# Square sums behind the chain at a phase boundary, and gated tiles in parts of 4, 6, 6, 6

## The chip, the cores and the metric

The kernel runs on one core of one Trainium2 chip. The metric is the device time of one execution in microseconds (us). The engines are PE (TensorE, the matmuls), DVE (VectorE), ACT (ScalarE), POOL (GpSimd) and SP (SyncE, which issues the loads of weights). Each works through its own instructions in order, and the order is fixed when the program is built.

## The reference

Two layers, each a feed-forward block, a mixing block and a second feed-forward block. 512 new prompt positions and 8 x 4 sampled positions go through the same weights; the width is 1024, all in float32.

```
def layer(x, ...):
    h = x + 0.5 * rmsnorm(swiglu(rmsnorm(x, norms[0]), w_ffn1_up, w_ffn1_down), norms[1])
    m, s_new, buf_new = mixer(rmsnorm(h, norms[2]), ...)      # retention and a short gated convolution
    h = h + rmsnorm(m, norms[3])
    h = h + 0.5 * rmsnorm(swiglu(rmsnorm(h, norms[4]), w_ffn2_up, w_ffn2_down), norms[5])

def swiglu(x, w_up, w_down):                                  # w_up: 1024 x 5632, w_down: 2816 x 1024
    gate, up = jnp.split(x @ w_up, 2, axis=-1)
    return (jax.nn.silu(gate) * up) @ w_down

def rmsnorm(x, g):
    return x * rsqrt(mean(x * x) + 1e-6) * g
```

## The kernel before

The 544 positions are the columns of every activation, in two halves of 272 (HALF); features lie on the 128 partitions, so the width of 1024 is 8 tiles (KT) and the inner width of 2816 is 22 tiles (FT). A float32 product is made of three matmuls, high part by high part, high by low and low by high. The high parts are copies made by ACT (`whi`, `xh`, `hh`, `oh`), the low parts are differences made by DVE (`wlo`, `xl`, `hl`, `ol`).

The work is a list of jobs in 6 phases: feed-forward, mixing, feed-forward, twice over. A plain `Job` is one output tile: 8 input tiles x 3 x 2 halves, 48 matmuls. A `Pair` computes two output tiles by seven block products of 4 x 3 matmuls, 84 instead of 96. It needs operands (sums and differences of quarters of the normalized input), which `build_ops` makes in four steps, two input tiles each, on DVE and ACT. Phases therefore begin with plain jobs. In a feed-forward phase the 22 gated tiles come in parts (PARTS): the gated tiles of a part, then 8 down tiles that take the part's tiles as inputs and add to the sums so far, which are copied into the PSUM bank first (`seed`, L194). Only the first part is done plainly, so its jobs are two for each gated tile (a gate, then an up) and then 8 down jobs. BUILD_AT says behind which jobs of that list the four builds are issued.

A boundary between phases is written out by hand. `boundary` fills a script with (time, function) pairs, sorts it, and that is the order on DVE, ACT and POOL (`play`); the times are only keys of the order. The order on PE and SP is that of the program too. Everything issued outside the scripts is placed on DVE, ACT and POOL by a planner, which may put such instructions among those of a script where it expects the engine to be idle.

In a boundary the last 5 jobs of a phase (TAIL) run half by half. While the second half of them runs on PE, the first half's residual `x` is finished by a chain on DVE and ACT (`chain`): scale y (L1165), add to x (L1169), high part of the next input (L1144, ACT), low part (L1150). Then PE starts the head, the first 5 jobs (HEAD) of the next phase, half by half: three jobs interleaved over the 8 input tiles, then two whole ones (`head_part`). While PE does the first half of the head, the second half's chain runs. The head runs on inputs that are not yet normalized; its results are copied from PSUM (`copy`, L1324) and are multiplied later by the reciprocal root of the mean square. For that each half needs a sum of squares over the 8 tiles of x: a square on ACT (L442) and an add on DVE (L444, the last one L448), then a matmul with ones on PE (L469) and `rstd`: a root on ACT (L481), three operations on DVE (L482 to L484). SUMS places the squares and adds in the script, RSTD_HEAD the two roots. After the second root `rest(0)` issues the evacuations of the first half (products with r, Silu, parts); `head_side` issues those of the second. `later_prep` makes the parts of the weights for the next jobs, five times in a boundary; its second step also frees the buffer of raw weights, on which SP's next load waits (three such buffers, L229).

PSUM has 8 banks, of which matmuls use 6 in a feed-forward phase and 5 in a mixing phase. A job takes one for each half, in the order in which they were given back.

The lines that count:

```
ev(SUMS[half] + 0.45 * f, lambda f=f: self.pre_sum(nxt, f, half, None, nc.vector))   # L1180
ev(RSTD_HEAD[half], lambda half=half: self.rstd([nxt["acc"][:, self.hs(half)]], half, nxt["r"], DM))   # L1344
ev(RSTD_HEAD[1] + 0.1, lambda: rest(0))   # L1345
ev((HEAD * half + max(3, n + 1)) * d + 0.1 + 0.3 * n * (n < 3), lambda n=n, half=half: copy(n, half))   # L1330, d = 2.78
jobs[at].after = lambda k=k: self.build_ops(ph, k)   # L574, for at in BUILD_AT
```

In the second half of the head the keys are 13.88 + 1.04 k for the interleaved steps on PE, 22.21 and 24.99 for the two whole jobs, and 22.31, 22.61, 22.91, 25.09 and 27.87 for the five copies.

Of the kernel before, what the change touches and what calls it, by code (L numbers as in the profile page):

```python
# [27 lines left out]
P = 128  # L28
KT = DM // P
FT = DFF // P  # L30
PARTS = [(0, 5), (5, 10), (10, 15), (15, 22)]
PLAIN_PARTS = 1
BUILD_AT = (6, 9, 11, 13)
CONV_PLAIN = 2
BUILD_MIX = (0, 2, 4, 5)
EPS = 1e-6
# [23 lines left out]
LAST_B = 1.2  # L60
ONES_B = 4.2
CHAIN_B = 5.0
SUMS = 11.0, 19.0
URGENT = 300
RSTD_HEAD = 17.5, 22.5


def log_gammas():
# [63 lines left out]
class Trunk:  # L132
# [362 lines left out]
    def ffn_jobs(self, ph):  # L495
# [4 lines left out]
        ph["y"] = {}  # L500
        for pi, (p0, p1) in enumerate(PARTS):
            hh = {}
# [51 lines left out]
            def dn(m, pi=pi, p0=p0, p1=p1, hh=hh):  # L554
                last = pi == len(PARTS) - 1

                def mv():
                    return [hh[i] for i in range(p0, p1)]

                def ev(half, ps):  # L560
                    if pi == 0 and half == 0:
                        ph["y"][m] = self.u("y")
                    if last:
                        self.y_out(ph, m, half, ps)
                    else:
                        nc.scalar.activation(out=ph["y"][m][:, self.hs(half)], in_=ps[:, :HALF], func=AF.Copy)

                return Job(down[l, n, m, :, p0 * P:p1 * P], mv, ev,
                           seed=(lambda half: ph["y"][m][:, self.hs(half)]) if pi else None)

            jobs += [dn(m) for m in range(KT)]
        self.no_ops(ph)
        for k, at in enumerate(BUILD_AT):
            jobs[at].after = lambda k=k: self.build_ops(ph, k)  # L574
# [582 lines left out]
    def chain(self, ev, at, ph, nxt, half):  # L1157

        nc, s = self.nc, self.hs(half)
        ts = {}  # L1160
        step = STEP if nxt else 0.8

        def scale(f):
            t = ts[f] = self.t("yg")
            nc.vector.tensor_tensor(out=t, in0=ph["y"][f][:, s], in1=ph["ry"][:, s], op=ALU.mult)  # L1165

        def add(f):
            x = self.x[f][:, s]
            nc.vector.tensor_tensor(out=x, in0=x, in1=ts.pop(f), op=ALU.add)  # L1169
            if nxt is None:  # L1170
                nc.sync.dma_start(out=self.a["y"][f, :, s], in_=x)

        for f in range(KT):
            t = at + step * f
            ev(t, lambda f=f: scale(f))
            ev(t + step + 0.4, lambda f=f: add(f))
            if nxt is not None:
                ev(t + step + 0.8, lambda f=f: self.pre_hi(nxt, f, half))
                ev(t + 2 * step + 0.8, lambda f=f: self.pre_lo(nxt, f, half))
                ev(SUMS[half] + 0.45 * f, lambda f=f: self.pre_sum(nxt, f, half, None, nc.vector))  # L1180

    def finish(self, ev, ph, d):

# [52 lines left out]
    def boundary(self, ph, nxt, i):  # L1236

        nc, script = self.nc, []  # L1240

        def ev(t, fn):
            script.append((t, len(script), fn))

        self.fill()
        self.x_changed = True
        mvs = [self.jobs[i + n].mv() for n in range(TAIL)]
        d = len(mvs[0]) * 3 * MM
        tb = -d * TAIL
        banks = {}  # L1250
        self.prep(i + TAIL + 1)
        self.tc.keep_in_program_order(nc.scalar.preload_act_table(AF.Abs_reciprocal_sqrt))
        ph["ry"] = self.u("ry")

        def seed(n, half):
            banks[n, half] = self.seeds(i + n, (half,))[0][1]

        def part(n, half):
            self.run_part(i + n, half, banks[n, half], 0, RSTD_AT if (n, half) == (0, 1) else KT)

        def between():
            self.rstd([ph["yacc"][:, self.hs(0)]], 0, ph["ry"], DM)
            self.run_part(i, 1, banks[0, 1], RSTD_AT)

        for half in range(2):
            at = -d * TAIL * (2 - half)
            for n in range(TAIL):
                ev(at + d * n - 0.9 * d, lambda n=n, half=half: seed(n, half))
                ev(at + d * n, lambda n=n, half=half: part(n, half))
                ev(at + d * (n + 1) + 0.1, lambda n=n, half=half: self.evac(self.jobs[i + n], half, banks[n, half]))  # L1270
        ev(tb + RSTD_AT * 3 * MM, between)
        if nxt is not None:
            self.pre_tiles(nxt)
            ev(-0.001, lambda: self.of_mix(nxt["kind"] == "mix"))
        self.chain(ev, tb + CHAIN_A, ph, nxt, 0)
        if nxt is None:
            self.finish(ev, ph, d)
        else:
            ev(LAST_B, lambda: ph["last"].pop()())
            ev(ONES_B, lambda: self.rstd([ph["yacc"][:, self.hs(1)]], 1, ph["ry"], DM))  # L1280
            self.chain(ev, CHAIN_B, ph, nxt, 1)
            V, G = nc.vector, nc.gpsimd
            self.head_script(ev, nxt, i + TAIL)
            for hi, lo in ((tb + d + 0.3, tb + d + 1.3), (tb + 2 * d + 0.3, tb + 2 * d + 1.3), (1.0, 2.0), (6.0, 7.0),
                           (14.0, 15.0)):
                self.later_prep(ev, hi, lo, V)
        self.play(script)
        if nxt is not None:
            self.head_side(nxt)
# [23 lines left out]
    def head_script(self, ev, nxt, i0):  # L1313

        nc = self.nc
        d = KT * 3 * MM
        if nxt["kind"] == "mix":
            self.mix_start(nxt)
        banks, out = [], []

        def copy(n, half):
            if half == 0:
                out.append(self.u("out"))
            nc.scalar.activation(out=out[n][:, self.hs(half)], in_=banks[half][n][:, :HALF], func=AF.Copy)  # L1324
            self.give(banks[half][n])

        for half in range(2):
            banks.append(self.head_part(ev, half * HEAD * d, nxt, i0, half))
            for n in range(HEAD):
                ev((HEAD * half + max(3, n + 1)) * d + 0.1 + 0.3 * n * (n < 3), lambda n=n, half=half: copy(n, half))  # L1330

        def rest(half):
            todo = []
            first = (3, 4) if nxt["kind"] == "mix" else ()
            for n in (*first, *(n for n in range(HEAD) if n not in first)):
                if n == 0 and first:
                    self.mix_tables(nxt, half)
                todo.append(self.jobs[i0 + n].evac(half, out[n][:, self.hs(half)]))
            for fn in todo:
                if fn:  # L1340
                    fn()

        for half in range(2):
            ev(RSTD_HEAD[half], lambda half=half: self.rstd([nxt["acc"][:, self.hs(half)]], half, nxt["r"], DM))  # L1344
        ev(RSTD_HEAD[1] + 0.1, lambda: rest(0))  # L1345
        nxt["rest"] = rest

    def head_side(self, nxt):
# [199 lines left out]
```

## Time and profile before

| | us |
|---|---|
| median of 3 runs | 2678.73 (2677.65 to 2682.8) |
| profiled execution | 2677.17 |
| its span, first to last instruction | 2675.3 |
| PE busy | 2628.3 (98%), 20718 matmuls |
| DVE busy | 1861.0 (70%) |
| ACT busy | 1354.0 (51%) |
| POOL busy | 237.3 (9%) |

The busy time of an engine is the time in which one of its instructions runs; PE's matmuls overlap, so that only its idle time is exact. A wait is the idle time of an engine before an instruction, with the instruction whose semaphore ended it behind the arrow. The granted clock is the share of its full rate that TensorE was allowed. Phases begin their heads on PE at about 6, 387, 955, 1334, 1713 and 2283 us.

### The profile page before, as it was taken

Reading aid. Unit: us, or ns where it says so; the run is one execution under the profiler, and the core shown is the slowest. Engines: PE = TensorE matmul, PEld = TensorE weight load, DVE = VectorE, ACT = ScalarE, POOL = GpSimd, SP = SyncE. Lnnn points to the kernel's source line nnn. Section 1 sums busy time; section 2 is a strip of 40 time slices with the busy share of each in tenths; the row PEclk is TensorE's granted clock in tenths of the full one; section 3 lists DMA queues with packets and bytes.
Section 4 is the critical chain, followed back from the end, with each engine's and each line's share of the span. In section 5 each row is a group of like instructions: output and inputs, shape, how many; then the busy total and the mean of one; then the engine's idle time right before and its main releaser. Section 6 shows DMA issues by size and latency. Waiting matters only on the chain. (4 is left out here: it accounts for less than half of the span.)

```text
span 2675.3 us, 50606 instructions
## 1 busy us (share of the span) xinstructions
PE 2628.3 (98%) x20718; PEld 2606.1 (97%) x20718; DVE 1861.0 (70%) x3213; ACT 1354.0 (51%) x2546; POOL 237.3 (9%) x375
## 2 busy tenths in 40 slices
PE   9999999999999999999999999999999999999998
PEld 9999998999999999999999999999999999999997
DVE  6756748677986487667488557587678764875673
ACT  6555554434553455555555555544345434655553
POOL 1000021222100100000100000211210001000002
PEclk9999999999999999999999999999999999999999
DMA  4233344333343432332432334343333433323332
GB/s 155 83 96 102 105 142 148 116 107 120 103 132 104 133 106 83 99 103 86 130 118 84 101 95 144 114 147 105 111 116 101 130 104 121 118 83 95 102 105 90
DMA packets 91977, 296.86 MB, mean 111 GB/s; under 512 B 12064, under 2 KB 16288, under 8 KB 91744
## 3 DMA queue, kind: packets, MB, share of 16 engines
q1 hardware_dynamic: 74592, 235.46, 28.9%
q0 software_dynamic: 17152, 58.16, 6.3%
q8 instruction: 162, 2.65, 0.4%
q14 instruction: 71, 0.58, 0.1%
HBM read 266.17 MB, written 27.41 MB: 110 GB/s over the span
## 5 line engine op out<-in xcount | busy, mean ns | idle before, releaser
L324 PE MATMUL banks<-oh,whi 128*128 128x272 f32 x2040 | 588.6, 289 | 3.0 <-ACT banks L194 1.6
L324 PE MATMUL banks<-oh,wlo 128*128 128x272 f32 x2040 | 587.9, 288 | 0.0
L324 PE MATMUL banks<-ol,whi 128*128 128x272 f32 x2040 | 586.6, 288 | 0.0
L324 PE MATMUL banks<-xh,whi 128*128 128x272 f32 x1600 | 455.2, 298 | 9.6 <-ACT out L1324 8.7
L324 PE MATMUL banks<-xl,whi 128*128 128x272 f32 x1600 | 442.4, 289 | 0.0
L252 ACT ACTIVATE whi<-raw 128x1024 fp32r<-128x1024 f32 (+2 forms) x273 | 253.5, 931 | 313.3 <-PE banks L324 248.4
L256 DVE TENSOR_TENSOR wlo<-raw,whi 128x1024 fp32r<-128x1024 f32 (+2 forms) x273 | 291.2, 1068 | 150.5 <-ACT whi L252 117.6
L324 PEld LDWEIGHTS banks<-oh,whi 128*128 128x128 f32 x2040 | 383.8, 188 | 6.4 <-ACT banks L194 2.8
L324 PE MATMUL banks<-hh,whi 128*128 128x272 f32 x1408 | 385.2, 289 | 0.1
L324 PE MATMUL banks<-hl,whi 128*128 128x272 f32 x1408 | 384.5, 288 | 0.2
L324 PEld LDWEIGHTS banks<-ol,whi 128*128 128x128 f32 x2040 | 384.5, 188 | 0.0
L324 PEld LDWEIGHTS banks<-oh,wlo 128*128 128x128 f32 x2040 | 383.9, 188 | 0.0
L324 PE MATMUL banks<-xh,wlo 128*128 128x272 f32 x1600 | 371.5, 289 | 0.4 <-DVE wlo L1395 0.4
L264 DVE TENSOR_TENSOR wlo<-s,whi 128x1024 fp32r<-128x1024 f32 x204 | 249.7, 1224 | 102.8 <-ACT whi L263 50.5
L324 PEld LDWEIGHTS banks<-xh,whi 128*128 128x128 f32 x1600 | 303.4, 190 | 13.2 <-ACT out L1324 10.0
L324 PE MATMUL banks<-hh,wlo 128*128 128x272 f32 x1408 | 313.3, 288 | 0.0
L324 PEld LDWEIGHTS banks<-xl,whi 128*128 128x128 f32 x1600 | 303.4, 190 | 2.1 <-DVE xl L1150 1.0
L263 ACT ACTIVATE whi<-s 128x1024 fp32r<-128x1024 f32 x204 | 214.8, 1055 | 141.3 <-PE banks L324 97.8
L324 PEld LDWEIGHTS banks<-xh,wlo 128*128 128x128 f32 x1600 | 267.9, 190 | 1.1 <-DVE wlo L1395 1.1
L324 PEld LDWEIGHTS banks<-hh,whi 128*128 128x128 f32 x1408 | 264.9, 188 | 0.9 <-ACT banks L194 0.8
L324 PEld LDWEIGHTS banks<-hl,whi 128*128 128x128 f32 x1408 | 264.8, 188 | 0.8 <-DVE hl L547 0.6
L324 PEld LDWEIGHTS banks<-hh,wlo 128*128 128x128 f32 x1408 | 229.6, 188 | 0.0
(246 smaller groups left out, 4993.3 us busy)
## 6 DMA issues: line engine op xcount, KB each, us to landing
raw<-in_w_up SPq DMA_DIRECT2D x173, 512.0 KB, 3.6
raw<-in_w_in SPq DMA_DIRECT2D x128, 512.0 KB, 3.6
raw<-in_w_down SPq DMA_DIRECT2D x96, 320.0 KB, 3.0
raw<-in_w_down SPq DMA_DIRECT2D x32, 448.0 KB, 4.0
xd<-x POOLq DMA_DIRECT2D x40, 272.0 KB, 2.7
x<-xd POOLq DMA_DIRECT2D x40, 272.0 KB, 4.9
s<-in_state_ret POOLq DMA_DIRECT2D x32, 256.0 KB, 3.5
out_ret_s<-s POOLq DMA_DIRECT2D x32, 256.0 KB, 2.9
```

The costliest lines, as they stand in the source:

```text
L252: self.nc.scalar.activation(out=hi[:, :n], in_=r[:, :n], func=AF.Copy)
L256: eng.tensor_tensor(out=lo[:, :n], in0=r[:, :n], in1=hi[:, :n].bitcast(F32), op=ALU.subtract)
L263: self.nc.scalar.activation(out=hi, in_=r, func=AF.Copy)
L264: self.nc.vector.tensor_tensor(out=lo, in0=r, in1=hi.bitcast(F32), op=ALU.subtract)
L324: self.nc.tensor.matmul(out=ps[:, :HALF], lhsT=w, rhs=x, start=start, stop=stop, skip_group_check=again)
```

## The change

The square sums of both halves, until now at 11.0 to 14.2 and 19.0 to 22.2 in the boundary's script, move to 17.6 to 18.0 and 18.2 to 18.6, that is behind the last step of the second half's chain (17.5). The fifth preparation of weights moves from 14.0 and 15.0 to 18.7 and 18.8. The first half's root moves from 17.5 to 18.3 and so behind one more step on PE; the second half's from 22.5 to 22.1 and so ahead of the two whole head jobs, and `rest(0)` from 22.6 to 22.15, ahead of the copy at 22.31. The parts of gated tiles become 4, 6, 6 and 6 instead of 5, 5, 5 and 7, the first of them plain; and the builds follow jobs 5, 6, 8 and 9 of a phase instead of 6, 9, 11 and 13.

```diff
@@ -28,9 +28,9 @@
-PARTS = [(0, 5), (5, 10), (10, 15), (15, 22)]
+PARTS = [(0, 4), (4, 10), (10, 16), (16, 22)]
 PLAIN_PARTS = 1
-BUILD_AT = (6, 9, 11, 13)
+BUILD_AT = (5, 6, 8, 9)
@@ -60,9 +60,9 @@
-SUMS = 11.0, 19.0
+SUMS = 17.6, 18.2
 URGENT = 300
-RSTD_HEAD = 17.5, 22.5
+RSTD_HEAD = 18.3, 22.1
@@ -1177,7 +1177,7 @@
-                ev(SUMS[half] + 0.45 * f, lambda f=f: self.pre_sum(nxt, f, half, None, nc.vector))
+                ev(SUMS[half] + 0.05 * f, lambda f=f: self.pre_sum(nxt, f, half, None, nc.vector))
@@ -1282,7 +1282,7 @@
             for hi, lo in ((tb + d + 0.3, tb + d + 1.3), (tb + 2 * d + 0.3, tb + 2 * d + 1.3), (1.0, 2.0), (6.0, 7.0),
-                           (14.0, 15.0)):
+                           (18.7, 18.8)):
@@ -1342,7 +1342,7 @@
-        ev(RSTD_HEAD[1] + 0.1, lambda: rest(0))
+        ev(RSTD_HEAD[1] + 0.05, lambda: rest(0))
```

## Rows read from the trace of the kernel before

**Rows 1.** The page, part 1: busy us (share of the span) and instructions of each engine.
```profile
PE 2628.3 (98%) x20718; PEld 2606.1 (97%) x20718; DVE 1861.0 (70%) x3213; ACT 1354.0 (51%) x2546; POOL 237.3 (9%) x375
```
**Rows 2.** Who waited for whom on PE: us in total, times, longest us.
```profile
PE banks L469 <- DVE acc L448: 15.4, 10, 1.6
PE banks L324 <- ACT out L1324: 8.7, 6, 2.8
...
PE banks L324 <- ACT banks L194: 1.6, 3, 0.7
```
**Rows 3.** Stretches: length, busy time (instructions) of five engines, clock, DMA share, GB/s.
```profile
1050.00:1250.00 200.00, 200.00 (x1597) 200.00 (x1597) 130.90 (x186) 105.87 (x200) 0.00 (x0) 1.00 0.33 96
...
49.50:52.90 3.40, 3.40 (x17) 3.40 (x17) 3.40 (x11) 2.71 (x7) 0.00 (x0) 0.50 0.00 0
1752.80:1756.10 3.30, 3.30 (x16) 3.30 (x16) 3.24 (x10) 0.30 (x1) 0.00 (x0) 0.50 0.00 0
425.60:429.00 3.40, 3.40 (x27) 3.40 (x28) 3.31 (x9) 0.74 (x3) 0.00 (x0) 1.00 0.02 6
```
**Rows 4.** Timeline of PE: start, length, instruction, [idle before, what ended it].
```profile
48.96 0.39 PE L324 MATMUL banks<-xh,whi 128*128 128x272 f32 x1 [2.52 <-ACT out L1324]
...
419.26 0.50 PE L469 MATMUL banks<-acc,ones 128*128 128x272 f32 x1 [1.60 <-DVE acc L448]
...
425.53 0.39 PE L324 MATMUL banks<-xh,whi 128*128 128x272 f32 x1 [2.29 <-ACT out L1324]
...
976.47 0.50 PE L469 MATMUL banks<-acc,ones 128*128 128x272 f32 x1 [1.57 <-DVE acc L448]
...
986.55 0.50 PE L469 MATMUL banks<-acc,ones 128*128 128x272 f32 x1 [1.58 <-DVE acc L448]
...
996.69 0.39 PE L324 MATMUL banks<-xh,whi 128*128 128x272 f32 x1 [0.40 <-ACT out L1324]
...
1744.41 0.50 PE L469 MATMUL banks<-acc,ones 128*128 128x272 f32 x1 [1.58 <-DVE acc L448]
...
1751.24 0.39 PE L324 MATMUL banks<-xh,whi 128*128 128x272 f32 x1 [2.83 <-ACT out L1324]
```
**Rows 5.** Timeline of DVE in the second boundary.
```profile
965.90 0.50 DVE L1150 SCALAR_TENSOR_TENSOR xl<-x,par,xh 128x272 fp32r<-128x272 f32 x1
...
967.01 0.50 DVE L1150 SCALAR_TENSOR_TENSOR xl<-x,par,xh 128x272 fp32r<-128x272 f32 x1
...
975.97 0.44 DVE L448 SCALAR_TENSOR_TENSOR acc<-sq,acc 128x272 f32<-128x272 f32 x1 [0.75 <-ACT sq L442]
...
981.85 3.17 DVE L444 TENSOR_TENSOR acc<-acc,sq 128x272 f32<-128x272 f32 x6
```
**Rows 6.** Timeline of ACT in the second boundary.
```profile
979.73 2.34 ACT L442 ACTIVATE sq<-x 128x272 f32<-128x272 f32 x7
...
991.88 1.28 ACT L513 ACT_TABLE_LOAD   x1
993.17 0.75 ACT L513 ACTIVATE sg<-sg 128x272 f32<-128x272 f32 x2
...
996.26 1.24 ACT L1324 ACTIVATE out<-banks 128x272 f32<-128x272 f32 x4
```
**Rows 7.** Timeline of DVE behind that boundary: a build, and the last plain job.
```profile
1001.24 0.78 DVE L587 SCALAR_TENSOR_TENSOR n<-x,par,r 128x544 f32<-128x544 f32 x1
...
1007.55 1.36 DVE L264 TENSOR_TENSOR ol<-t,oh 128x544 fp32r<-128x544 f32 x2
...
1020.95 0.79 DVE L520 TENSOR_TENSOR tu<-banks,r 128x272 f32<-128x272 f32 x2 [4.50 <-PE banks L324]
...
1023.10 0.79 DVE L526 TENSOR_TENSOR hl<-tu,hh 128x272 fp32r<-128x272 f32 x2
```
**Rows 8.** The stretch from that boundary's second root to the first Pair's operands.
```profile
991.10:1047.80 56.70, 56.30 (x449) 56.08 (x448) 47.56 (x97) 32.13 (x67) 0.00 (x0) 1.00 0.24 70
```
**Rows 9.** Timeline of DVE in the first boundary: the first half's last two low parts.
```profile
392.61 0.91 DVE L1150 SCALAR_TENSOR_TENSOR xl<-x,par,xh 128x272 fp32r<-128x272 f32 x2
```

## The prediction

> **What bounds the kernel now.** I read the page's first part, then who waited for whom on PE, then each PE wait in the timeline with the DVE and ACT rows around it. The page says PE is busy 98% of a span of 2675.3 us [rows 1]: time can only come from matmuls that go away and from PE's own waits. The waits view shows few of these [rows 2]: 15.4 us for the square sums of the next phase's input, 2 at each of the 5 boundaries between phases, some 1.5 us each; 8.7 us for the copies that empty the PSUM banks of the head tiles; 1.6 us for seeds. All PE waits over 60 ns add up to 34 us, and no rate can be won elsewhere: in 200 us of undisturbed feed-forward work 1597 matmuls run, 0.1252 us each, at granted clock 1.00 [rows 3]. One price hides behind the waits. After the waits of 2.52 and 2.83 us [rows 4] the granted clock fell to 0.50 (1.2 GHz) for 3.4 us, with 17 and 16 matmuls in a stretch where 27 run at 1.00 (2.4 GHz); after the wait of 2.29 us it stayed at 1.00 [rows 3]. Ten lost matmuls are 1.3 us on top of such a wait.
>
> **The change part by part**, against the profiled execution (2677.17 us, that is 1.56 us under the median of the runs shown).
>
> (a) Fewer matmuls. A gated tile done plainly is 2 jobs of 48, a Pair is 7 products of 12, so 84. Each of the 4 feed-forward phases turns one tile from plain to Pair: 4 x 12 x 0.1252 = -6.0 us. Down tiles keep their count, only the parts differ. This is certain, as PE has nothing else in these stretches.
>
> (b) Sums behind the chain. In the second boundary the rows are these [rows 5]: low parts come every 1.11 us (965.90, 967.01) until the sums of the first half and two weight splits cut in, and the last add of the first half starts only at 975.97; PE reads it 0.50 us later, after a wait of 1.57 [rows 4]. With the sums behind the chain the last low part ends near 973.4 (965.90 and 7 steps, the last ones shorter as nothing is left to scale) and the last high part leaves ACT free at 972.8. Squares take 0.32 us each (7 in 2.34 [rows 6]), adds on one accumulator 0.545 us from start to start (6 in 3.17 [rows 5]): first add 973.6, seventh 976.85, PE reads at 977.35. That is 0.9 later than now, but PE has by then done one more step of 9 matmuls, 1.1 us: gain 0.25. The second half: two adds, then 0.75 to the reciprocal root, 0.4, three DVE operations of 0.475 (to 979.9), five adds, last one at 982.0, PE at 982.5 with 48 matmuls still to do, so the head ends at 982.5 + 0.37 + 6.0 = 988.9; now it is 986.55 + 0.37 + 24 x 0.1252 = 989.9. Gain 1.0 per boundary, 5.0 in all. So both waits stay, shorter only by what no longer cuts in. Bounds: 0 (one more weight split, 1.07 us in the mean by the page's part 5, lands among the adds) to 3.1 each (both waits gone). The split put at 18.8 frees its raw buffer some 6 us later, and SP's next weight load waits as long; that load is for the fourth job after the head, over 18 us away, and lands in 3.6 us by the page's part 6: nothing.
>
> (c) Order of bank copies. The second root and everything queued behind it (the first half's evacuations) now stand ahead of ACT's copy of the first head tile; until now that one copy ran early and the other four came behind, at 996.26 [rows 6]. PE reaches the first job behind the head 6.4 us after the second sum (0.37 and 48 matmuls) and needs the copy at 6.6; today that is 3.4 us (24 matmuls), since the fourth tile now stands behind the sum too, and waits there with it.
> Before the two mixing phases the bank came 6.3 and 6.8 us after the sum (425.53 - 419.26; 1751.24 with its sum at 1744.41), and PE waited 2.29 and 2.83 [rows 4]; with 3.0 us more to do these fall to about 0.2 each: -4.7, and -1.3 for the half clock. Bounds 0 to 5.1.
> Before the three feed-forward phases a sixth bank and the early copy let PE pass, and it waited only 0.40 a job later, for a copy ready 10.1 us after the sum (996.69 - 986.55 [rows 4]). Now the first job itself needs that copy, at 6.6. With one weight split (1.15) and one Silu of the second half (0.35) fewer ahead of it I take it ready at 8.6: 2.0 of wait instead of 0.4, three times, +4.9. Bounds: 0 to 3.5, and 1.3 more where it grows like the two long waits.
> At the start of the kernel the same wait is 2.52 [rows 4]; I take 2.0 there and a clock that stays up: -0.5 and -1.3.
> Behind the root on ACT stands a table switch for Silu, 1.28 us at 991.88, and the Silu starts 11 ns after its end [rows 6]. The Trainium skill (ScalarE: Activation LUTs, What ACT_TABLE_LOAD costs) puts every switch at about 2.66 us, of which 1.38 is a drain; by it the four new or kept waits would each be 1.38 us longer, +5.5 to the sum, as an estimate from that page. The row shows no such drain here, and the sum goes by the row.
>
> (d) Operands for the Pairs. One build takes 5.1 us of DVE (1001.24 to 1008.91 less 2.5 of other work [rows 7]). Builds now follow jobs 5, 6, 8 and 9 of the phase. Between PE's end of job 5 and of job 7 lie 96 matmuls, 12.0 us; DVE has to do the evacuation of an up tile (2.1), a split (0.6), build 0 (5.1), a gate (0.7), build 1 (5.1) and another split (0.6), 14.2 us. So the evacuation of job 7 starts about 2.1 late, its first low part is ready 4.1 to 4.7 after the job's end (2.6 now: 1020.9 to 1023.5 [rows 7]), and the first down tile reaches its fourth input after 18 matmuls, 2.3 us, where now it had 24, 3.0 us: a wait of 1.75 in each phase, +7.0. Bounds: 0 (job 7 goes ahead of the build) to 4.5 (the whole second build ahead of it).
> From job 5's end to the first Pair DVE has 36.4 us of work (two up tiles 4.2, a gate 0.7, four builds 20.2, eight splits 4.8, the first Pair's sums and splits 6.5) in 36.1 of PE (96 and 192 matmuls); the wait above and the later products' slack of 1.5 to 9 us take up the rest: 0.
>
> (e) Parts of 6. Last parts of 7 wait 1.6 us for seeds in all [rows 2], where 448 KB loads hold ACT; the 384 KB loads should shorten that: -1.0, bounds -2.0 to +3 (the last tile's low half is due 0.75 us earlier). The tail before a boundary loses 15 matmuls, 1.9 us of cover for the first half's chain; its last low part ended at 393.5 [rows 9], about 2.0 ahead of PE's step, so that cover is just used up, and what it may cost (0.6) is swallowed by the wait in (b): 0.
>
> Sum: -6.0 - 5.0 - 4.7 - 1.3 + 4.9 - 0.5 - 1.3 + 7.0 - 1.0 = -7.9, so 2669.3 for the profiled execution and 2670.8 for the median: 2671.
>
> **The rivals.**
> Slower: the first Pair comes late. In the like stretch before (991.1 to 1047.8) DVE was busy 47.56 of 56.70 us, idle 9.1 for want of inputs [rows 8]. If idle time recurs in proportion, 36/57 of 9.1 or 6 us, the first Pair starts 6 late instead of 1.75 in 4 phases: +17, 2688. It decides once DVE cannot finish the fourth build some 7 us ahead of the Pair. For it: builds of one phase run on each other's heels on ACT and DVE. Against: half of that idle, 4.5 us, was one piece in which DVE waited for PE alone [rows 7], with nothing left to do.
> Faster: neither new wait appears, the bank copies being ready at 6.6 and job 7's evacuation ahead of build 1: -6.0 and -7.0 from -7.9, 2658. For it: nothing on PE forces these orders. Against: the order on ACT is fixed by hand.
> It doesn't do what it says: the sums come no earlier and the long bank waits stay, so (b), the 4.7 and the 1.3 fall away: +11, 2682. For it: adds alone on DVE run at 0.545 and not 0.35 us.
> Table switch: it holds ACT a second 1.28 us ahead of the copies, three times before feed-forward phases and at the start: +5.1, 2676. The row at 993.17 speaks against it [rows 6]. The Trainium skill (ScalarE: Activation LUTs, What ACT_TABLE_LOAD costs) gives a switch such a second part.
>
> **How the numbers follow.** Forecast 0.50 (its own range 2664 to 2677), late Pair 0.16, no new wait 0.17, not done 0.14, table 0.03. The range 2657 to 2687 takes in the fast case and nearly all of the slow one. A change within 0.2% (2673.4 to 2684.1) can't be told from none. Faster: three quarters of the forecast and all of the fast case, 0.55; slower: most of the late Pair and a little of the third, 0.15; within, 0.30.
>
> **What would show it.** (a) matmuls: 20670 instead of 20718, Pairs of 84 in parts of 6. (b) two waits for the sums at each boundary still there, together some 0.8 to 1.0 shorter, no weight split between chain and sums. (c) waits for the bank copies before mixing phases under 0.5, before feed-forward phases near 2 at the first job behind the head, and clock 1.00 after all of them. (d) a wait of 1 to 2.5 us in the first down tile for low parts, none at the first Pair. (e) seed waits under 1 us. It is wrong if PE waits at a first Pair, if the clock falls after a bank wait, or if the sums' waits are gone.

## The result, and the profile after

The changed kernel takes 2695.80 us (median of 4, 2693.57 to 2701.30), the kernel before 2679.07 beside it: ratio 1.0063, 95% interval [1.0044, 1.0083]. It is slower by 16.7 us, where 2671 and a range of 2657 to 2687 were forecast. The profiled execution took 2697.59 us, 20.4 more than that of before.

The page of the kernel after, part 1 (columns as in [rows 1]):

```profile
PE 2634.7 (98%) x20670; PEld 2609.0 (97%) x20670; DVE 1875.5 (70%) x3225; ACT 1362.6 (51%) x2558; POOL 237.0 (9%) x375
```

The 48 matmuls are gone, and PE is busy 6.4 us longer all the same, in part because matmuls at half clock last longer. Who waited for whom on PE, after (us in total, times, longest; against [rows 2]):

```profile
PE banks L324 <- ACT out L1324: 13.1, 6, 2.8
PE banks L469 <- DVE acc L448: 10.7, 10, 1.2
PE banks L324 <- ACT hh L525: 7.4, 8, 1.4
PE banks L324 <- ACT banks L194: 3.7, 7, 1.4
PE banks L324 <- DVE xl L1150: 2.4, 3, 0.8
```

The sum waits fell by 4.7 (5.0 were forecast). The bank waits grew from 8.7 to 13.1, the first down tiles wait 7.4 for their last operand, and seeds and the last low parts of three boundaries add 4.5. The PE timeline after, one place of each kind (against [rows 4]):

```profile
42.79 0.39 PE L324 MATMUL banks<-xh,whi 128*128 128x272 f32 x1 [1.82 <-ACT out L1324]
...
425.39 0.39 PE L324 MATMUL banks<-xh,whi 128*128 128x272 f32 x1 [1.16 <-ACT out L1324]
...
979.31 0.73 PE L469 MATMUL banks<-acc,ones 128*128 128x272 f32 x2 [1.21 <-DVE acc L448]
...
984.56 0.73 PE L469 MATMUL banks<-acc,ones 128*128 128x272 f32 x2 [1.14 <-DVE acc L448]
...
994.31 0.59 PE L324 MATMUL banks<-xh,whi 128*128 128x272 f32 x1 [2.75 <-ACT out L1324]
...
1016.56 0.39 PE L324 MATMUL banks<-hh,whi 128*128 128x272 f32 x1 [0.45 <-ACT hh L525]
1018.80 0.39 PE L324 MATMUL banks<-hh,whi 128*128 128x272 f32 x1 [1.37 <-ACT hh L525]
...
1764.66 0.39 PE L324 MATMUL banks<-xh,whi 128*128 128x272 f32 x1 [1.82 <-ACT out L1324]
```

What ScalarE did ahead of the wait at 994.31 (start, length, instruction; the second sum was read at 984.56):

```profile
985.32 0.40 ACT L481 ACTIVATE y<-banks 128x272 f32<-128x272 f32 x1 [1.36 <-PE banks L469]
985.61 1.05 ACT L252 ACTIVATE whi<-raw 128x1024 fp32r<-128x1024 f32 x1
988.35 0.63 ACT L252 ACTIVATE whi<-raw 128x512 fp32r<-128x512 f32 x1 [1.68 <-DMA raw<-in_w_down]
989.52 1.28 ACT L513 ACT_TABLE_LOAD   x1 [0.53 <-DVE sg L512]
990.81 0.43 ACT L513 ACTIVATE sg<-sg 128x272 f32<-128x272 f32 x1
...
993.88 1.52 ACT L1324 ACTIVATE out<-banks 128x272 f32<-128x272 f32 x5
```

All five copies stand at 993.88, behind the evacuations. PE had stopped at 991.56, with no bank left. Meanwhile VectorE, which finishes the root, had three weight splits (L256) to do:

```profile
984.42 2.35 DVE L256 TENSOR_TENSOR wlo<-raw,whi 128x1024 fp32r<-128x1024 f32 x2
986.69 0.43 DVE L482 SCALAR_TENSOR_TENSOR yq<-banks,y 128x272 f32<-128x272 f32 x1
987.04 1.22 DVE L256 TENSOR_TENSOR wlo<-raw,whi 128x1024 fp32r<-128x1024 f32 x1
988.17 0.44 DVE L483 TENSOR_TENSOR yq<-yq,y 128x272 f32<-128x272 f32 x1
988.64 0.44 DVE L484 SCALAR_TENSOR_TENSOR r<-yq,y 128x272 f32<-128x272 f32 x1
```

No split stands among the sums now, but the root came 4.5 us after the second sum, as late as in before (986.55 to 991.08). At the first down tile VectorE has the second build's low parts (L264) among job 7's evacuation, one for one:

```profile
1014.56 0.44 DVE L520 TENSOR_TENSOR tu<-banks,r 128x272 f32<-128x272 f32 x1
1014.91 0.72 DVE L264 TENSOR_TENSOR ol<-t,oh 128x544 fp32r<-128x544 f32 x1
1015.54 0.44 DVE L524 TENSOR_TENSOR tu<-tu,sg 128x272 f32<-128x272 f32 x1
1015.89 0.72 DVE L264 TENSOR_TENSOR ol<-t,oh 128x544 fp32r<-128x544 f32 x1
1016.54 0.44 DVE L526 TENSOR_TENSOR hl<-tu,hh 128x272 fp32r<-128x272 f32 x1
```

Last, stretches behind waits (columns as in [rows 3]):

```profile
994.20:997.60 3.40, 3.29 (x14) 3.29 (x15) 3.31 (x9) 3.40 (x11) 0.00 (x0) 0.50 0.44 141
1018.80:1022.20 3.40, 3.31 (x24) 3.11 (x25) 3.40 (x8) 2.07 (x5) 0.00 (x0) 1.00 0.55 154
65.80:69.20 3.40, 3.37 (x14) 3.19 (x15) 3.39 (x7) 2.07 (x5) 0.00 (x0) 0.51 0.55 154
1765.50:1768.90 3.40, 3.40 (x17) 3.40 (x16) 3.34 (x9) 2.12 (x4) 0.00 (x0) 0.51 0.00 0
2335.60:2339.00 3.40, 3.40 (x17) 3.40 (x16) 1.27 (x3) 0.72 (x3) 0.00 (x0) 0.50 0.27 77
2359.50:2362.90 3.40, 3.40 (x17) 3.40 (x17) 3.40 (x9) 2.07 (x5) 0.00 (x0) 0.50 0.33 131
```

A stretch at 0.50 (1.2 GHz) does 14 to 17 matmuls where 27 run at 1.00 (2.4 GHz). After the start of the kernel, before had two of them; after has seven (two not shown are at 1379.90 and 2332.20; that at 2335.60 follows the second of these), so five more at some 1.4 us each: 7 us.

Where the 20.4 us lie, from the start of the first product of each stretch to that of the next, less its matmuls at 0.1253 us (the rows of heads hold waits for low parts too, 0.9 to 1.0 us at three boundaries, which belong to (e), and that of the mixing heads one of 1.0 us for masked scores):

| stretch | forecast | measured |
|---|---|---|
| 48 matmuls fewer | -6.0 | -6.0 |
| head at the start | -1.8 | -1.9 |
| two mixing heads (b and c) | -8.0 | -1.3 |
| three feed-forward heads (b and c) | +1.9 | +10.6 |
| four first down tiles (d) | +7.0 | +15.1 |
| other Pairs and down tiles (e) | -1.0 | +3.8 |
| sum | -7.9 | +20.3 |

### The profile page after: what moved, and what is told of

Same layout as the page of the kernel before. It is cut to its first block, busy times and chain, and to the rows that moved or that the text cites. A ratio compares the mean times of both kernels' runs of the same rounds, so it can differ in the third digit from the quotient of the medians.

```text
span 2695.8 us, 50542 instructions
## 1 busy us (share of the span) xinstructions
PE 2634.7 (98%) x20670; PEld 2609.0 (97%) x20670; DVE 1875.5 (70%) x3225; ACT 1362.6 (51%) x2558; POOL 237.0 (9%) x375
## 5 line engine op out<-in xcount | busy, mean ns | idle before, releaser
L324 PE MATMUL banks<-oh,whi 128*128 128x272 f32 x2120 | 613.2, 289 | 5.3 <-ACT banks L194 3.7
L324 PE MATMUL banks<-oh,wlo 128*128 128x272 f32 x2120 | 610.5, 288 | 0.0
L324 PE MATMUL banks<-ol,whi 128*128 128x272 f32 x2120 | 610.0, 288 | 0.0
L324 PE MATMUL banks<-xh,whi 128*128 128x272 f32 x1472 | 423.5, 300 | 14.7 <-ACT out L1324 13.1
L324 PE MATMUL banks<-xl,whi 128*128 128x272 f32 x1472 | 410.2, 291 | 2.4 <-DVE xl L1150 2.4
L324 PEld LDWEIGHTS banks<-oh,wlo 128*128 128x128 f32 x2120 | 399.3, 188 | 0.0
L256 DVE TENSOR_TENSOR wlo<-raw,whi 128x1024 fp32r<-128x1024 f32 (+2 forms) x265 | 281.0, 1063 | 145.7 <-ACT whi L252 113.0
L324 PE MATMUL banks<-xh,wlo 128*128 128x272 f32 x1472 | 346.3, 290 | 0.5 <-DVE wlo L256 0.3
L264 DVE TENSOR_TENSOR wlo<-s,whi 128x1024 fp32r<-128x1024 f32 x212 | 259.2, 1224 | 124.2 <-PE banks L324 59.0
L324 PEld LDWEIGHTS banks<-xh,whi 128*128 128x128 f32 x1472 | 281.2, 191 | 18.5 <-ACT out L1324 14.4
L324 PEld LDWEIGHTS banks<-xl,whi 128*128 128x128 f32 x1472 | 281.5, 191 | 4.1 <-DVE xl L1150 3.0
L324 PEld LDWEIGHTS banks<-xh,wlo 128*128 128x128 f32 x1472 | 249.2, 191 | 1.2 <-DVE wlo L1395 0.7
```

The lines of the kernel that those rows point to most:

```text
L256: eng.tensor_tensor(out=lo[:, :n], in0=r[:, :n], in1=hi[:, :n].bitcast(F32), op=ALU.subtract)
L264: self.nc.vector.tensor_tensor(out=lo, in0=r, in1=hi.bitcast(F32), op=ALU.subtract)
L324: self.nc.tensor.matmul(out=ps[:, :HALF], lhsT=w, rhs=x, start=start, stop=stop, skip_group_check=again)
```

## The experiments

Each was timed beside the kernel before; the ratio is to that.

| kernel | us | before | ratio, 95% interval |
|---|---|---|---|
| boundary only | 2690.37 | 2680.73 | 1.0038 [1.0025, 1.0052] |
| parts only | 2695.12 | 2680.73 | 1.0053 [1.0038, 1.0068] |
| after, copies first | 2686.55 | 2680.73 | 1.0022 [1.0013, 1.0031] |
| after, wait filled | 2695.74 | 2680.73 | 1.0051 [1.0035, 1.0068] |
| after, build 1 later | 2724.30 | 2679.86 | 1.0169 [1.0154, 1.0184] |
| boundary only, copies first | 2668.85 | 2679.86 | 0.9959 [0.9945, 0.9974] |
| copies first, build 1 later | 2711.16 | 2679.86 | 1.0120 [1.0103, 1.0136] |
| before, sums behind the chain | 2681.07 | 2679.86 | 1.0005 [0.9995, 1.0014] |
| copies first, builds at 5, 7, 9, 11 | 2689.54 | 2678.63 | 1.0039 [1.0024, 1.0054] |
| boundary, copies first, split back | 2673.10 | 2678.63 | 0.9977 [0.9967, 0.9987] |
| before, copies first | 2666.93 | 2678.63 | 0.9958 [0.9943, 0.9973] |
| copies first, builds at 5, 7, 10, 12 | 2674.56 | 2679.16 | 0.9980 [0.9970, 0.9989] |
| before, copies first, parts of after | 2674.03 | 2679.16 | 0.9981 [0.9971, 0.9990] |

**Each half of the change alone.** The boundary's new order with the parts of before:

```
-PARTS = [(0, 4), (4, 10), (10, 16), (16, 22)]
-BUILD_AT = (5, 6, 8, 9)
+PARTS = [(0, 5), (5, 10), (10, 15), (15, 22)]
+BUILD_AT = (6, 9, 11, 13)
```

> The changed kernel with the parts (5, 5, 5, 7) and the build places (6, 9, 11, 13) of before; what is new at the boundaries stays. Theory (two causes that add: the new order at the boundaries +7.5 us against before, the new parts and build places +13 us): 2686 us, 2683 to 2689; the waits of 2.75 us for the first bank behind the head stay at three boundaries, the waits of 0.5 and 1.4 us for low parts in the first down tiles are gone, matmuls back at 20718. Rival A, the boundary's new order is the whole loss and the new parts only save their 6 us of matmuls: 2700 or more. Rival B, the boundary's order gains as forecast (sums 5 us, the bank waits about even) and all of the loss lies in the parts: 2676 or less.

And the reverse, made on the kernel of before (the same four lines turned round):

> The kernel of before with only the parts (4, 6, 6, 6) and the build places (5, 6, 8, 9) of the change. Theory: the first down tile of each of the 4 feed-forward phases waits some 3 to 4 us in all (half clock included), the Pairs some 1.3 us per phase, less 6 us of matmuls: +13 us against before, 2692, 2687 to 2695. Rival A (the whole loss at the boundaries): 2673, faster by the 6 us of matmuls. Rival B (the loss in the first down tile comes of the late head, and not of the builds): 2676 or less, with no wait in the first down tile.

2690.37 and 2695.12, 1.4 and 0.1 us over the upper ends of the theory's ranges: both halves lose, and neither rival that puts the loss into one half holds. They do not add: 9.6 and 14.4 make 24, the change cost 16.7. Waits and ScalarE of the boundary alone:

```profile
PE banks L324 <- ACT out L1324: 20.4, 6, 5.5
```

```profile
986.41 1.06 ACT L252 ACTIVATE whi<-raw 128x1024 fp32r<-128x1024 f32 x1 [2.60 <-DMA raw<-in_w_up]
...
992.84 1.52 ACT L1324 ACTIVATE out<-banks 128x272 f32<-128x272 f32 x5
```

Here the bank waits are longer than in the change itself. ScalarE stood 2.60 us in front of a weight split whose load had not landed, with the copies queued behind it. The parts alone have these waits in the first down tile, where the sum waits are as before:

```profile
PE banks L324 <- ACT hh L525: 7.4, 8, 2.4
...
PE banks L324 <- DVE hl L526: 4.2, 4, 1.1
```

**The copies first.** The evacuation of the first half 0.8 us later in the order of events, so that three copies precede it on ScalarE:

```
-        ev(RSTD_HEAD[1] + 0.05, lambda: rest(0))
+        ev(RSTD_HEAD[1] + 0.85, lambda: rest(0))
```

> The changed kernel with one place moved: the evacuation of the first half behind the head is issued 0.8 us later in the order of events, so behind three of ScalarE's five copies of head tiles. Theory (the bank waits of 2.75 us at the first job behind the head come of the order on ScalarE, and the half clock behind them of the wait): these waits fall under 0.5 us at the three feed-forward heads, each also gives back 1.6 us of half clock, 13 us in all there, some 3 more at the other heads; nothing is lost behind them: 2680 us, 2677 to 2685. Rival A (the copies are late because the sums are late; the order on ScalarE only changes who waits): within 3 us of the changed kernel, 2693 to 2698. Rival B (the evacuation that is now later becomes the wait of the job after): some 5 us gained, 2689 to 2692, with a wait for hh or xh a job later.

2686.55, between the theory and rival B. The waits for the copies are gone from the list altogether. ScalarE at the same head:

```profile
986.41 0.40 ACT L481 ACTIVATE y<-banks 128x272 f32<-128x272 f32 x1 [1.36 <-PE banks L469]
986.70 0.97 ACT L1324 ACTIVATE out<-banks 128x272 f32<-128x272 f32 x3
```

So the order on ScalarE made these waits. Not all of it is kept, as two waits grew (the first was 7.4, the second 0.9):

```profile
PE banks L324 <- ACT hh L525: 9.2, 8, 1.4
PE banks L1001 <- DVE l L986: 4.4, 2, 2.3
```

PE is earlier at the first down tile, and the operand is as late as ever: two of the tiles lose 2.1 us more each. The second is for the low part of the masked scores in the mixing phases (L986), which VectorE makes; that it comes later because of the evacuation that was moved was not tested.

The same line moved in the boundary-only kernel:

> The changed kernel with the parts and build places of before and with the evacuation of the first half issued 0.8 us later, behind three of ScalarE's copies. Theory (with the parts of before undone and the copies first, the shorter sum waits and the gain at the two mixing heads are left): the parts are worth 10 to 13 us, so 2686.5 less these: 2674 to 2677, with no bank wait above 1 us behind a head and no wait in a first down tile. Rival A (in the kernel with only the parts undone the bank waits were 4.6 to 5.5 us because weights arrive late, not because of the order on ScalarE): waits of 2 us or more stay at the three feed-forward heads, 2680 to 2686. Rival B (the new place of the sums costs as much as it gains): 2679 to 2682, same as before.

2668.85, better than the theory had it and 21.5 us under the kernel without that line; no wait for the copies is left, and no first down tile waits. This beats both kernels. ScalarE still stood 1.86 us in front of a late load at this head, until 984.79, but the three copies that PE needed stood ahead of it.

The same order in the kernel of before, with no other part of the change:

```
-        ev(RSTD_HEAD[1] + 0.1, lambda: rest(0))
+        ev(RSTD_HEAD[1] + 0.45, lambda: rest(0))
```

> The kernel of before with one place moved: the evacuation of the first half behind a head is issued 0.35 us later in the order of events, behind three of ScalarE's copies instead of one. Theory (the bank waits behind a head, 8.7 us in the trace of before, and the half clock behind two of them, 3 us, come of this order alone, and that is what the mended kernel gained): waits for these copies under 0.5 us, 2670, 2667 to 2673. Rival A (the evacuation that follows is late by as much, and the next product waits for it): 2676 to 2681 with waits for l L986. Rival B (without the sums behind the chain the copies come too late all the same): 2678 to 2681.

2666.93, the fastest of all, and not to be told from the kernel just above. The bank waits are gone, with them both stretches at half clock; its sum waits are those of before:

```profile
PE banks L469 <- DVE acc L448: 15.2, 10, 1.6
```

So with the banks free in time, the whole new order of sums and split gains nothing over this: 12.2 instead of 15.2 us of sum waits, but 4.6 instead of 1.8 at the masked scores and two stretches at half clock (from 441.71 and 1766.08 on) where this kernel has none.

**The wait filled.** After, with 20 matmuls that nothing reads behind the three heads:

```
+        if nxt["kind"] == "ffn" and i0:
+            ev(2 * HEAD * d, lambda: self.fill_pe(nxt))
...
+        for n in range(20):
+            self.nc.tensor.matmul(out=ps[:, :HALF], lhsT=self.ones_r, rhs=nxt["xh"][0][:, self.hs(0)],
+                                  start=n == 0, stop=n == 19)
```

> The changed kernel with 20 matmuls more, whose results nothing reads, behind the head of each of the three feed-forward phases that follow another phase, 2.5 us at the rate of the others, which is the length of the wait there. Theory (the fall to half clock follows from the idle of TensorE): the granted clock stays at 1.00 behind these three heads, and 1.6 to 3.2 us of each comes back, 2689 to 2692 us, while the first job starts at the same time as before. Rival A (the clock falls for another reason, and the 60 matmuls only lie in the wait): no change, 2694 to 2697. Rival B (the fill is not hidden, since the bank that it takes is one that is waited for): slower by up to 7 us.

2695.74, as after. The time is rival A's, the mechanism is the theory's. Stretches of this kernel, behind the head and behind the wait in the first down tile:

```profile
993.20:996.60 3.40, 3.21 (x26) 2.98 (x25) 3.29 (x9) 3.21 (x10) 0.00 (x0) 1.00 0.55 142
1019.10:1022.50 3.40, 3.35 (x13) 3.16 (x14) 3.37 (x7) 2.07 (x6) 0.00 (x0) 0.50 0.52 154
```

At the head the clock now stayed at 1.00, as at the other two heads with a fill; the three give back 5.4 us from start to start. But behind the first down tile's wait of 1.36 us, practically that of after, where the clock stayed up at 1018.80, it fell to 0.50, and the three first down tiles behind such heads lose 5.0 us more. In these three phases after has five stretches of 3.4 us at half clock, four at the heads; this kernel has five too, all in the first down tiles. The half clock was moved by 26 us and not removed. One execution stands against one here, and the number of such stretches varies without a fill too: the first phase, which has none, shows three in this kernel and one in after.

**Sums and split.** Before, with the sums alone moved:

```
-SUMS = 11.0, 19.0
-RSTD_HEAD = 17.5, 22.5
+SUMS = 17.6, 18.2
+RSTD_HEAD = 18.3, 22.5
-                ev(SUMS[half] + 0.45 * f, lambda f=f: self.pre_sum(nxt, f, half, None, nc.vector))
+                ev(SUMS[half] + 0.05 * f, lambda f=f: self.pre_sum(nxt, f, half, None, nc.vector))
```

> The kernel of before with only the square sums put behind the whole chain (and the first root behind them, where it has to stand); the weight split, the second root and the evacuation behind it keep their places, and so do the parts. Theory (the sums gain by themselves some 0.5 to 1.0 us per boundary, as the shorter waits in the changed kernel show): 2677, 2674 to 2680. Rival A (the sums then run late on VectorE, and the copies behind the root with them, so that bank waits grow): 2683 or more. Rival B (no difference, the split now cuts in elsewhere): 2679 to 2682 with sum waits of 15 us.

2681.07: no difference, rival B in time, though its 15 us of sum waits became 17.6. The two waits of a boundary become one of twice the length:

```profile
PE banks L469 <- DVE acc L448: 17.6, 5, 3.7
```

In the kernel with 2668.85 us, only the weight split put back:

```
-                           (18.7, 18.8)):
+                           (14.0, 15.0)):
```

> The kernel with the boundary's new order, the parts of before and the copies first (2669 us), with only the place of the one weight split put back from 18.7 to 14.0. Theory (the split among the chain delays the sums, and that is why the sums alone gained nothing): sum waits up from 12.2 to some 17 us, 2674, 2672 to 2677. Rival (the split's place does not matter, as its load is not needed soon and VectorE has the time): 2667 to 2670.

2673.10, as the theory had it, 4.2 us more. Sum waits, and the stretch behind one of 3.45 us:

```profile
PE banks L469 <- DVE acc L448: 17.0, 5, 3.5
```

```profile
976.40:979.80 3.40, 3.40 (x14) 3.17 (x14) 2.32 (x6) 1.99 (x6) 0.00 (x0) 0.50 0.01 2
```

The clock fell behind all five of these waits. With the sums behind the chain, it is the split's place, among the chain or behind it, that makes them late or early; the split moved without the sums was not run.

**Where the builds stand.** After, with the second build behind job 7:

```
-BUILD_AT = (5, 6, 8, 9)
+BUILD_AT = (5, 7, 8, 9)
```

> The changed kernel with one number moved: the second build of Pair operands stands behind job 7, the last up tile, and no more ahead of it. Theory (the first down tile waits because the second build, 5 us of VectorE, goes ahead of job 7's evacuation; VectorE has some 7 us left before the first Pair, as the trace with the copies first shows): the waits in the first down tiles vanish with the half clock behind them, 3.1 to 4.6 us in each of 4 phases, and none comes at the first Pair: 2681, 2679 to 2685. Rival A (the work is conserved: what is saved at the first down tile is paid at the first Pair): 2691 to 2697, with a wait for ol or oh at the first Pair. Rival B (the wait is that of the late head, which also delays job 7): unchanged waits in the first down tile, 2693 or more.

And this together with the copies first:

> The changed kernel with both places mended: the evacuation of the first half behind three of ScalarE's copies, and the second build behind job 7. Theory (the loss is these two orders, and the rest of the change gains): the 4.4 to 5.3 us in each first down tile of the kernel with the copies first go, 16 to 20 us in all: 2668, 2665 to 2673, so some 12 us under the kernel before; no bank wait over 0.5 us behind a feed-forward head, none over 0.5 us in a first down tile. Rival A (conserved work: the first Pair is late instead): 2680 to 2686. Rival B (evacuations behind the head are now so late that job 5's or 6's operands wait): half of the gain, 2675 to 2680.

2724.30 and 2711.16, far from every number written down but the open end of one rival, 2693 or more with unchanged waits in the first down tile. Those waits are gone; a new and longer one stands a few down jobs later. Waits and ScalarE of the first of the two:

```profile
PE banks L324 <- ACT y L566: 26.3, 8, 5.0
```

```profile
1040.42 0.43 ACT L599 ACTIVATE b<-n 128x272 fp32r<-128x272 f32 x1 [2.93 <-DVE n L587]
...
1043.11 1.06 ACT L263 ACTIVATE whi<-s 128x1024 fp32r<-128x1024 f32 x1 [1.33 <-DVE t L597]
...
1046.63 1.80 ACT L566 ACTIVATE y<-banks 128x272 f32<-128x272 f32 x6
```

Builds behind jobs 7, 8 and 9 follow each other at once. On ScalarE their rounding copies wait for VectorE, and the copies that free the banks of the down results (L566) stand behind them: six at once, 5 us late. So what was saved comes back, as rival A said, but at the banks, not at the first Pair, and as more.

With the copies first, builds further apart, (5, 7, 9, 11) and then (5, 7, 10, 12):

> The changed kernel with the evacuation of the first half behind three of ScalarE's copies, and the builds behind jobs 5, 7, 9 and 11 (the kernel with the copies first had 5, 6, 8 and 9). Theory (the builds cost when they follow each other closely: their operands' copies on ScalarE wait for VectorE, and what stands behind them there, job 7's evacuation or the banks of the first down job's results, waits too; a gap of two down jobs between builds lets both pass): the 20 us in the four first down tiles fall to under 6, none is lost at the first Pair: 2670, 2666 to 2675. Rival A (two builds on three jobs is still too dense: ScalarE's copies of down results come late and TensorE waits for banks): 2680 to 2700 with waits for y L566. Rival B (the last build is now too late for the first Pair): 2676 to 2690 with a wait for ol or oh there.

> The changed kernel with the copies first and the builds behind jobs 5, 7, 10 and 12 (two kernels before this one had 5, 6, 8, 9: 2686.6, and 5, 7, 9, 11: 2689.5). Theory (ScalarE takes its work in order: the copies of down results, which free the banks, stand behind the rounding copies of a build that wait for VectorE; with three down jobs between builds each copy comes before the next build): the wait of 3.2 us for y L566 in the first down tile and its half clock fall to under 1 us, and the last build, which ends some 1 us after TensorE reaches the first Pair, costs about that: 2674, 2670 to 2679. Rival A (VectorE's work between job 5 and the first Pair does not fit in 36 us with four tiles, wherever the builds stand): what is saved at the banks returns as a wait of 3 us or more at the first Pair, 2684 to 2692. Rival B (the banks are kept by something else than the builds): the waits for y L566 stay, 2686 to 2692.

The first gave 2689.54, a miss (rival A): one wait of 3.2 us for L566 in each phase, 12.9 us in all. The second gave 2674.56, as the theory had it: no wait for L566 or for hh left, some 2 us lost in the first six Pairs of each feed-forward phase. Two places moved turn the change from 16.7 us slower into 4.6 us faster.

The parts of after and builds at (5, 7, 10, 12) in the kernel with 2666.93 us:

> The kernel of before with the copies first behind the heads (2667 us), with the parts (4, 6, 6, 6) of the change and builds behind jobs 5, 7, 10 and 12. Theory: 6 us of matmuls fewer, some 1.3 us of seed waits and up to 1 us at each first Pair more in 4 phases: 2667, 2664 to 2672, so the parts can be had at no loss, and no gain, once the builds stand apart. Rival A (the work does not fit): 2675 to 2685. Rival B (all 6 us come through): 2661.

2674.03: 7 us slower than without them, over the theory's 2672 and just under rival A. Against the kernel without them the first six Pairs of a phase lose 2.0 to 3.4 us, 9.9 in all, the first down tiles 1.8; that is more than the 6 us of matmuls.

## Why the prediction was wrong

(a) Right: 20670 matmuls, 6.0 us.

(b) Right for the two sum waits, in size and, as far as tested, in reason: both stayed and got 4.7 us shorter together. The sums were read at 979.31 and 984.56 in a head that began 2.0 us later (956.80 instead of 954.80), where 977.35 and 982.5 were forecast for the earlier start. The sums alone gained nothing (2681.07), and with the sums moved the split is worth 4.2 us. What failed is the "nothing" for the loads. I asked when a load's weights are needed, 18 us later, and not what stands on ScalarE behind the split that waits for it. In the boundary-only kernel a split that waited 2.60 us for its load stood ahead of the copies, and in the change itself this happened at the mixing heads.

(c) The mechanism was right, the sizes were not, and this is the step that cost most: the mixing and feed-forward heads lie 15.4 us over their forecast. At the mixing heads I let the bank come 6.3 and 6.8 us after the second sum, as in before, and so wanted 0.2 of wait each. It came 7.9 and 8.5 after (425.39 - 417.47; 1764.66 - 1756.12), and waits of 1.16 and 1.82 were left, with half clock behind the second. SP issues a load 0.02 to 0.03 us after a VectorE split ends and frees a buffer. In before such a split ended just ahead of the second sum, at 418.86 (the sum was read at 419.26):

```profile
418.89 3.42 SPq L229 DMA_DIRECT2D raw<-in_w_in  x3
```

```profile
422.39 1.06 ACT L252 ACTIVATE whi<-raw 128x1024 fp32r<-128x1024 f32 x1 [1.42 <-DMA raw<-in_w_in]
```

In after the splits stand behind the last add, so the load goes 1.1 us behind the sum (417.47), and the table switch, the Silu and all five copies wait with it on ScalarE:

```profile
418.57 2.95 SPq L229 DMA_DIRECT2D raw<-in_w_in  x3
```

```profile
422.24 1.07 ACT L252 ACTIVATE whi<-raw 128x1024 fp32r<-128x1024 f32 x1 [2.67 <-DMA raw<-in_w_in]
...
1761.52 1.06 ACT L252 ACTIVATE whi<-raw 128x1024 fp32r<-128x1024 f32 x1 [3.29 <-DMA raw<-in_w_in]
```

The one moved split is not to blame for this wait by itself: at the first mixing head it is 1.79 us in the kernel with 2668.85 us and 1.82 with the split put back.

At feed-forward heads I took the copy ready 8.6 us after the second sum, and PE needing it at 6.6. PE ran out of work 7.0 after the sum and went on 9.75 after it (994.31 - 984.56), so 2.75 of wait instead of 2.0. I had counted one weight split and one Silu fewer ahead of the copies. The Silu was right; but VectorE had three splits between the sum and the root, as many as in before, and ScalarE four between its part of the root and the copies (985.61 to 992.49) where before had two. I expected the clock to stay up, but it fell at all three: the waits there grew by 7.2 us from start to start (4.9 forecast), and four stretches at half clock cost 5.9 more, for which the sum had nothing. The head at the start came out as forecast, 1.82 of wait and a clock that stayed up.

The table switch was one of 1.28 us (989.52), and the Silu follows at 990.81. The second part that the Trainium skill (ScalarE: Activation LUTs, What ACT_TABLE_LOAD costs) gives a switch, a drain of about 1.38 us, doesn't show here either.

(d) The wait was named with its place and its idle time: 1.75 forecast (its own rows, 4.1 to 4.7 less 2.3, give 1.8 to 2.4), 0.45 + 1.37 = 1.82 shown, caused as described by the second build among job 7's evacuation; with that build moved behind job 7 the wait is gone. The view names the high part (L525) of that evacuation, not the low part. What it cost was mis-sized: 3.1 us where the clock stayed up and 4.3 to 4.6 where it fell. The idle time of this view runs from the drawn end of the matmul before, which is 0.28 to 0.39 us long while its successor could start 0.125 after it; and the products behind that need the low part start late too. From start to start the five late products at 1016.56 to 1019.50 lose 3.06 us.

(e) Wrong in sign. Loads of 384 KB did not shorten the seed waits (3.7 instead of 1.6), and the tail's missing cover, which I let the sum wait swallow, shows as 2.4 us for low parts (L1150).

Of the rivals, the late first Pair came nearest in time (2688) and not in mechanism: no Pair was late, as the first down tile was. The measured sum lies 28.2 us over the forecast one. Some 10 of these are seven falls to half clock, 1.4 us each: a fall was priced at the waits that would go and at none of the waits that would come. The rest is in the waits themselves, at the heads, in the first down tiles and in (e).

## What to carry to other kernels

On an engine that takes its work in order, ask of each moved instruction not when its result is needed but what stands behind it while it waits; the copy that frees a bank goes ahead of everything that can wait for a load or for another engine. Price a new wait by its start-to-start loss and by the half clock that may follow it, and not by its idle time alone. Where work is packed closer, look for the next in-order queue: the same builds showed as a late operand, as a full bank and as late Pairs, depending on where they stood.

## What the hardware showed that was not expected

The granted clock went to 0.50 behind a wait of 1.38 us at 65.83 and not behind one of 1.37 at 1018.80 of the same execution; with the head's wait before it filled, it did fall at 1019.15. So the length of the wait alone did not decide here, and what did was not settled: where falls went from the heads they came at the next wait. In the fastest kernel, whose waits behind the start are at most 1.6 us each, no stretch at half clock is left, and its mean clock is 0.998; after has 0.993.
